# Two merge units moved forward in the list of stage 1 of a hybrid decoder block

## The chip, the core and the metric

The kernel runs on one core of one Trainium2 chip. The metric is the device time of one execution in microseconds (us). Times of single instructions are in us or ns, counted from the start of the profiled span.

## What is computed

A decoder block works on x of 1024 tokens by 1024 channels in float32. Cut to the parts that matter here:

```python
h = rmsnorm(x, norm_mix_g)
q, kv, nsa_g, u, merge_g = split(h @ w_in)         # 512, 768, 24, 512, 2048 columns
y_a = nsa(q, rope(q), compress(k_c), compress(v_c), k_s, v_s, k_w, v_w, gates) @ w_attn_branch
y_ssm = gelu(s5(u, ...))                           # 32 groups, state 64, a scan over the tokens
y_b = (y_ssm @ w_ssm_val) * sigmoid(y_ssm @ w_ssm_gate)
g_a, g_b = split(merge_g)
x = x + (sigmoid(g_a) * y_a + sigmoid(g_b) * y_b) @ w_out
x = x + square(relu(rmsnorm(x) @ w_up)) @ w_down
return rmsnorm(x, norm_final_g)
```

The merge gates `merge_g` are a product of the normed input with 2048 columns of `w_in`. They depend on nothing else and are not read before the two branches are joined.

## The kernel before

The kernel has three stages. Nearly every large product is made of three matmuls (high by high, low by high, high by low halves of float32 operands), so each weight is first cast to its high half on ACT (L111) and its low half is found by a subtraction (L112), on POOL for most weights.

**Stage 1** norms the input, transposes it into eight tiles hT, makes the u projections and then works through a list of units, the string DENSE (L50, `dense`, L618 to L638):
- `s`: one of eight batches of four state-space groups (`s5_prep`, `s5_main`). Tables and weights are made on VectorE, with sines on ACT, four transposes (pw, L513), small products (L520, L541, L542, L557 to L560), a scan on VectorE, and GELU on VectorE (L570 to L574). The batch is given to the scheduler with a priority 1200 instructions ahead (HP).
- `k`: one projection for the compressed keys or values (`kv_unit`).
- `c`: one compression MLP (`compress`), with a priority 600 ahead (HC).
- `a`, `b`: the query projection and the key, value and gate projection of one of the two key heads (`qkv_half`): eight blocks of 24 matmuls into tile ps_a, each block evacuated on ACT, rotated on POOL (L384 to L387), transposed (L402, L432) and split on ACT and VectorE (L410, L411, L429, L434, L435).
- `m`: one merge unit (`merge_steps`, L139 to L157): one weight of 128 by 1024, two halves of 24 matmuls of 512 columns each (L150, tile ps_m), a tanh on ACT (L156, tile mst) and a store to mg_d (L157). It needs nothing of VectorE.

The list gives the order in which instructions are handed to a scheduler. It keeps a time model of the engines and lets each engine take, of the instructions that are ready, the one of the best priority; priorities follow the order of the list, save for the units that stand ahead. What results is a fixed order for every engine and for SP's DMA queue. Sixteen merge units exist in all. N1 = 5 of them stand in DENSE; the first three (ND) use the three banks of the pool dps, the others the single bank of mps. Ten more (NM) are fillers of stage 2, handed out two matmuls at a time between attention products, the first 48 matmuls (PRE) ahead of it; the last one opens stage 3. Weights come through two raw slots (NR) and four weight slots.

**Stage 2** is the attention of 16 pairs of key head and block. Its first loads (L672 qT, L681 kT, L683 vt) wait for SBUF that stage 1 has given up. **Stage 3** joins the branches and runs the MLP, with a hand-written order.

Of the kernel before, what the change touches and what calls it, by code (L numbers as in the profile page):

```python
# [46 lines left out]
ATQ, MGQ, DB, MI, PW = 1, 1, 1, 0, 6  # L47
DP1, SP1, XP1, NKQ, NVV, NQT, QL = 3, 2, 2, 2, 2, 3, 1
ND3, E4, S4B, AHEAD = 5, 5, 2, 5
DENSE = 'ssksmkcssscsabasbmmmm'  # L50
N1 = DENSE.count("m")
MORDER = [f for i in range(8) for f in (i, 8 + i)]
EPS = 1e-6
# [12 lines left out]
def hybrid_block(ctx: ExitStack, tc: tile.TileContext, a: dict, out: bass.AP, dbg=None):  # L66
# [108 lines left out]
    with ExitStack() as st1:  # L175
# [446 lines left out]
        def dense(x):  # L622
            i = count[x] = count.get(x, -1) + 1
            if x == "s":
                with tc.high_priority(offset=HP) if HP else ExitStack():
                    s5_main(i, s5_prep(i))
            elif x == "k":
                kv_unit(i)
            elif x == "c":
                with tc.high_priority(offset=HC) if HC else ExitStack():  # L630
                    compress(i)
            elif x == "m":
                merge_unit(MORDER[i], dps if i < ND else None)
            else:
                qkv_half(i, "ab".index(x))

        for x in DENSE:
            dense(x)  # L638
# [869 lines left out]
```

## Time and profile before

| what | value |
|---|---|
| median of 3 runs | 1561.51 us (1561.37 to 1562.64) |
| the profiled execution | 1559.56 us, span 1557.5 us |
| TensorE (PE) busy | 1513.8 us, 97% |
| VectorE (DVE) busy | 1053.8 us, 68% |
| ACT, POOL busy | 747.7 us, 446.4 us |

Busy time of PE is the union of its matmuls, whose ends are modelled. PEld is the weight load, which overlaps PE. In a timeline each row is start, length, engine, line, operation, output and inputs, shapes and count; a bracket names the idle time just before it and the instruction that ended it. In a table by stretch each row is the stretch, its length, then busy time and count of each engine, the granted TensorE clock, the busy share of the DMA engines and GB/s.

### The profile page before, as it was taken

Reading aid. Unit: us, or ns where it says so; the run is one execution under the profiler, and the core shown is the slowest. Engines: PE = TensorE matmul, PEld = TensorE weight load, DVE = VectorE, ACT = ScalarE, POOL = GpSimd, SP = SyncE. Lnnn points to the kernel's source line nnn. Section 1 sums busy time; section 2 is a strip of 40 time slices with the busy share of each in tenths; the row PEclk is TensorE's granted clock in tenths of the full one; section 3 lists DMA queues with packets and bytes.
Section 4 is the critical chain, followed back from the end, with each engine's and each line's share of the span. In section 5 each row is a group of like instructions: output and inputs, shape, how many; then the busy total and the mean of one; then the engine's idle time right before and its main releaser. Section 6 shows DMA issues by size and latency. Waiting matters only on the chain. (4 is left out here: it accounts for less than half of the span.)

```text
span 1557.5 us, 22364 instructions
## 1 busy us (share of the span) xinstructions
PE 1513.8 (97%) x7938; PEld 1272.8 (82%) x7938; DVE 1053.8 (68%) x1867; ACT 747.7 (48%) x1548; POOL 446.4 (29%) x431
## 2 busy tenths in 40 slices
PE   7999999999999999999999979999999999999996
PEld 6789999888888888888888867888888778888885
DVE  7995977358987978565542568555555467757576
ACT  6343444347677766532221455555555444444452
POOL 3114535211011011000000034444444355445453
PEclk9999999999999999999999999999999999999998
DMA  6434455652123111363342214444443677533533
GB/s 234 134 95 156 142 165 183 180 159 63 59 59 115 39 54 49 135 233 108 122 159 84 82 44 172 164 149 149 149 149 122 197 272 235 174 109 109 188 109 122
DMA packets 113503, 211.07 MB, mean 136 GB/s; under 512 B 14704, under 2 KB 49520, under 8 KB 113392
## 3 DMA queue, kind: packets, MB, share of 16 engines
q1 hardware_dynamic: 104176, 192.87, 37.9%
q10 hardware_dynamic: 9216, 16.78, 3.1%
q8 instruction: 62, 1.02, 0.3%
q14 instruction: 49, 0.40, 0.1%
HBM read 139.36 MB, written 68.16 MB: 133 GB/s over the span
## 5 line engine op out<-in xcount | busy, mean ns | idle before, releaser
L1373 PE MATMUL pg<-w 128*128 128x512 f32 x1344 | 309.0, 392 | 4.3 <-DVE w L1246 3.4
L1373 PEld LDWEIGHTS pg<-w 128*128 128x128 f32 x1344 | 253.3, 189 | 59.8 <-DVE w L1246 5.3
L150 PE MATMUL ps_m<-hT,w 128*128 128x512 f32 x768 | 215.3, 400 | 0.4 <-ACT mst L156 0.3
L1244 POOL TENSOR_TENSOR w<-raw,w 128x512 fp32r<-128x512 f32 x112 | 153.3, 1372 | 161.0 <-ACT w L1243 159.8
L1243 ACT CAST w<-raw 128x512 fp32r<-128x512 f32 x112 | 69.5, 620 | 165.3 <-PE pg L1373 104.4
L150 PEld LDWEIGHTS ps_m<-hT,w 128*128 128x128 f32 x768 | 130.6, 188 | 21.5 <-ACT mst L156 0.8
L1062 PE MATMUL pa<-T,w 128*128 128x512 f32 x576 | 141.7, 395 | 1.1 <-POOL w L1079 1.1
L1079 POOL TENSOR_TENSOR w<-raw,w 128x1024 fp32r<-128x1024 f32 (+1 forms) x48 | 101.1, 2108 | 104.1 <-ACT w L1078 104.1
L1062 PEld LDWEIGHTS pa<-T,w 128*128 128x128 f32 x576 | 108.1, 188 | 26.7 <-POOL w L1079 1.6
L1246 DVE TENSOR_TENSOR w<-xy,w 128x512 fp32r<-128x512 f32 x64 | 87.2, 1371 | 47.4 <-ACT w L1245 32.1
L112 POOL TENSOR_TENSOR w<-raw,w 128x1024 fp32r<-128x1024 f32 (+1 forms) x27 | 71.1, 2636 | 162.4 <-ACT w L111 162.4
L769 ACT ACTIVATE p<-s_ps,sst 128x640 f32<-128x640 f32 (+7 forms) x128 | 90.0, 707 | 23.5 <-PE pt L804 13.4
L127 POOL TENSOR_TENSOR rstd<-ss,neghalf 128x1 f32<-128x1 f32 x16 | 8.8, 551 | 293.1 <-DVE ss L125 293.1
L1246 DVE TENSOR_TENSOR w<-z,w 128x512 fp32r<-128x512 f32 x48 | 59.6, 1243 | 43.4 <-ACT w L1245 41.5
L763 PE MATMUL s_ps<-kT,qT 128*128 128x512 f32 (+3 forms) x384 | 85.8, 337 | 0.2
L804 PE MATMUL pt<-ident,p 128*128 128x128 f32 x528 | 83.8, 275 | 2.1 <-DVE pl__5079 L708 1.0
L766 DVE CUSTOM_DVE_ANT_0 s_ps<-s_ps,cmask 128x256 f32<-128x256 f32 (+7 forms) x96 | 63.8, 676 | 19.6 <-PE s_ps L763 19.1
L119 PE MATMUL ps_a<-w,hT 128*128 128x256 f32 (+1 forms) x256 | 74.8, 292 | 0.0
L118 PE MATMUL ps_a<-w,hT 128*128 128x256 f32 (+1 forms) x256 | 74.6, 291 | 0.0
L120 PE MATMUL ps_a<-w,hT 128*128 128x256 f32 (+1 forms) x256 | 74.0, 289 | 0.0
L763 PEld LDWEIGHTS s_ps<-kT,qT 128*128 128x128 f32 x384 | 63.7, 189 | 11.5 <-ACT p L769 1.3
L804 PEld LDWEIGHTS pt<-ident,p 128*128 128x128 f32 x528 | 62.4, 140 | 12.4 <-PE s_ps L763 1.3
(1432 smaller groups left out, 3497.5 us busy)
## 6 DMA issues: line engine op xcount, KB each, us to landing
raw<-act_d SPq DMA_DIRECT2D x56, 512.0 KB
raw<-w_up SPq DMA_DIRECT2D x32, 512.0 KB
act_d<-ts SPq DMA_DIRECT2D x16, 1024.0 KB
raw<-w_mg SPq DMA_DIRECT2D x16, 512.0 KB
mg_d<-mst SPq DMA_DIRECT2D x32, 256.0 KB
act_d<-e SPq DMA_DIRECT2D x16, 512.0 KB
xy<-w_down ACTq DMA_DIRECT2D x32, 256.0 KB
z<-w_down ACTq DMA_DIRECT2D x32, 256.0 KB
```

The costliest lines, as they stand in the source:

```text
L118: T.matmul(ps, lhsT=wh, rhs=xh, start=first and i == 0, stop=False)
L119: T.matmul(ps, lhsT=wl, rhs=xh, start=False, stop=False)
L120: T.matmul(ps, lhsT=wh, rhs=xl, start=False, stop=last and i == n - 1)
L150: m = T.matmul(ps, lhsT=w[:, e, ks], rhs=hT[k][:, r, hs], start=k == 0 and i == 0, stop=k == KD - 1 and i == 2)
L763: T.matmul(s_ps[:, o:o + hi - lo], lhsT=qT[:, 2 + hp * 2 + j, :], rhs=kT[g, br, hf][:, e, lo - hf * 512:hi - hf * 512], start=e == 0, stop ...
L769: A.activation(pp[j][:, 0:w], row, AF.Exp, scale=-1.0, bias=st[:, 0, j:j + 1], accum_out=st[:, 2, j:j + 1])
L804: T.transpose(pt[:, i, j, :], c[hp, br][j][:, (i0 + i) * P:(i0 + i + 1) * P], ident)
L1062: T.matmul(ps, lhsT=w[:, e, ks], rhs=x[:, k], start=first and k + i == 0, stop=k == 3 and i == 2, skip_group_check=not first)
L1079: G.tensor_tensor(w[:, 1, i * n:i * n + n], x, f32(w[:, 0, i * n:i * n + n]), op=ALU.subtract)
L1244: G.tensor_tensor(w[:, 0, 1], raw, f32(w[:, 0, 0]), op=ALU.subtract)
L1246: V.tensor_tensor(w[:, 1, 1], t, f32(w[:, 1, 0]), op=ALU.subtract)
L1373: T.matmul(ps, lhsT=w[:, 0, e, bs], rhs=w[:, 1, r], start=first and q + i == 0, stop=q == 15 and i == 2, skip_group_check=not first)
```

## The change

Two of the four letters m at the end of DENSE move forward: one to the place after the fourth s, one to the place after the sixth s. The number of letters m stays 5, and their numbering, their banks and everything else in the kernel stay as they are.

```diff
@@ -47,7 +47,7 @@
 ATQ, MGQ, DB, MI, PW = 1, 1, 1, 0, 6
 DP1, SP1, XP1, NKQ, NVV, NQT, QL = 3, 2, 2, 2, 2, 3, 1
 ND3, E4, S4B, AHEAD = 5, 5, 2, 5
-DENSE = 'ssksmkcssscsabasbmmmm'
+DENSE = 'ssksmkcsmssmcsabasbmm'
 N1 = DENSE.count("m")
 MORDER = [f for i in range(8) for f in (i, 8 + i)]
 EPS = 1e-6
```

## Rows read from the trace of the kernel before

**Rows 1.** The page: busy time of TensorE, and its granted clock in 40 slices

```profile
PE 1513.8 (97%) x7938; PEld 1272.8 (82%) x7938; DVE 1053.8 (68%) x1867; ACT 747.7 (48%) x1548; POOL 446.4 (29%) x431
...
PEclk9999999999999999999999999999999999999998
```

**Rows 2.** Table by stretch: stretch, length, busy by engine, clock, DMA share, GB/s

```profile
113.70:155.00 41.30, 41.30 (x350) 40.41 (x348) 22.93 (x46) 18.01 (x45) 16.52 (x33) 1.00 0.49 149
155.00:223.00 68.00, 64.68 (x536) 62.59 (x536) 63.42 (x119) 30.40 (x87) 33.84 (x65) 1.00 0.53 157
223.00:265.00 42.00, 42.00 (x355) 41.34 (x355) 28.84 (x68) 20.38 (x62) 17.50 (x45) 1.00 0.53 164
265.00:301.00 36.00, 36.00 (x195) 30.28 (x194) 14.24 (x22) 9.92 (x20) 13.67 (x19) 1.00 0.59 170
301.00:337.00 36.00, 35.62 (x182) 29.65 (x181) 14.59 (x63) 16.21 (x50) 6.46 (x6) 1.00 0.67 201
```

**Rows 3.** Timeline of TensorE: its waits after 113 us, to 340 us

```profile
192.35 0.44 PE L432 MATMUL pk<-ident,k 128*128 128x128 f32 x2 [1.26 <-DVE k L429]
...
197.01 0.66 PE L513 MATMUL pw<-ident,wq 128*128 128x128 f32 x4 [1.96 <-DVE x L546]
...
336.38 0.73 PE L150 MATMUL ps_m<-hT,w 128*128 128x512 f32 x2 [0.34 <-ACT mst L156]
```

**Rows 4.** Timeline of VectorE: long instructions, and one of ordinary length

```profile
99.86 2.52 DVE L509 TENSOR_TENSOR wq<-wq,wq 128x512 f32<-128x512 f32 x1
...
117.84 2.44 DVE L474 TENSOR_TENSOR ang<-th,cidx 128x512 f32<-128x512 f32 x1
...
184.99 0.28 DVE L429 COPY k<-k 128x256 f32<-128x256 f32 x1
...
189.74 2.56 DVE L429 COPY k<-k 128x256 f32<-128x256 f32 x1
...
193.15 3.00 DVE L574 SCALAR_TENSOR_TENSOR gz<-gz,gy 128x512 f32<-128x512 f32 x1
```

**Rows 5.** Timeline of POOL: the subtractions for weights, 99 to 196 us

```profile
99.32 2.50 POOL L112 TENSOR_TENSOR w<-raw,w 128x1072 fp32r<-128x1072 f32 x1 [14.57 <-ACT w L111]
...
115.57 4.15 POOL L112 TENSOR_TENSOR w<-raw,w 128x1072 fp32r<-128x1072 f32 x1 [8.98 <-ACT w L111]
...
151.44 2.37 POOL L112 TENSOR_TENSOR w<-raw,w 128x1024 fp32r<-128x1024 f32 x1 [1.59 <-ACT w L111]
...
154.37 2.39 POOL L112 TENSOR_TENSOR w<-raw,w 128x1024 fp32r<-128x1024 f32 x1
...
189.23 2.92 POOL L112 TENSOR_TENSOR w<-raw,w 128x1072 fp32r<-128x1072 f32 x1
...
192.58 3.03 POOL L112 TENSOR_TENSOR w<-raw,w 128x1072 fp32r<-128x1072 f32 x1
```

**Rows 6.** Timeline of TensorE: first projection, first merge of the tail, first attention

```profile
113.72 0.28 PE L118 MATMUL ps_a<-w,hT 128*128 128x256 f32 x1
...
265.24 0.40 PE L150 MATMUL ps_m<-hT,w 128*128 128x512 f32 x1
...
301.36 0.61 PE L724 MATMUL pc_ps<-kvc,qT 128*128 128x128 f32 x4
...
308.84 5.74 PE L150 MATMUL ps_m<-hT,w 128*128 128x512 f32 x24
```

**Rows 7.** Timeline of ACT: the cast of the second query weight

```profile
80.59 1.05 ACT L111 CAST w<-raw 128x1024 fp32r<-128x1024 f32 x1 [1.58 <-PE ps_k L120]
```

**Rows 8.** Timeline of SP's queue: stage 1's last stores, stage 2's first load

```profile
277.88 8.09 SPq L157 DMA_DIRECT2D mg_d<-mst  x2
...
289.88 2.46 SPq L566 DMA_DIRECT2D y_d<-gz  x4
...
294.17 0.32 SPq L672 DMA_DIRECT2D qT<-q_d  x1
```

**Rows 9.** Table by stretch, the merge matmuls (L150) alone: PE, PEld busy

```profile
265.00:301.00 36.00, 28.91 (x119) 22.15 (x120) 1.00 0.59 170
301.00:337.00 36.00, 29.86 (x125) 22.55 (x123) 1.00 0.67 201
```

## The prediction

> **What bounds the kernel now.** I began with the busy shares and the slices of the page [rows 1]. TensorE is busy for 1513.8 of 1557.5 us and the granted clock is nine tenths of full speed (2.4 GHz) or more in 39 of the 40 slices, so the span holds 1557.5 - 1513.8 = 43.7 us in which TensorE does nothing. The change moves TensorE's work and takes none away. It can gain only idle time, and only idle time that the moved units can fill.
>
> Next comes the table by stretch for the end of the first stage [rows 2], to see which idle time that is. From 113.7 to 155 us TensorE is full and VectorE is busy 22.93 of 41.30 us. From 155 to 223 us VectorE is the tight engine, 63.42 of 68.00 us, and TensorE idles 68.00 - 64.68 = 3.32 us. From 223 to 301 us TensorE is full again, although VectorE has only 14.24 us of work in the last 36 us. From 301 to 337 us it idles 0.38 us. So in the whole reach of the change TensorE idles 3.7 us. The rest of the 43.7 us lies at the launch, at the hand-over to the MLP and at the tail, which the order of stage 1 does not touch.
>
> Then the TensorE timeline says where the 3.3 us are: two waits, 1.26 us before the key transposes and 1.96 us before a state-space transpose, both released by VectorE [rows 3], 3.22 us together. VectorE's timeline shows why it was late: a key copy that takes 0.28 us at 184.99 takes 2.56 us at 189.74, and a GELU product takes 3.00 us at 193.15 [rows 4]. Both stretched instructions lie against a POOL subtraction for the low halves of the next weights (189.23 and 192.58 us, 2.92 and 3.03 us long) [rows 5]. The trace has that pattern before as well: 2.52 us at 99.86 and 2.44 us at 117.84 on VectorE [rows 4], beside POOL's subtractions at 99.32 and 115.57 [rows 5], and there TensorE did not wait.
>
> That is a lock in the rows: a VectorE instruction of 0.28 us ends when POOL's ends. The Trainium skill, page "SBUF — State Buffer", section "Who interferes with whom", states it as an exclusive lock of a port pair that VectorE and GpSimd share, held for a whole instruction; the trace agrees (2.56 against 0.28 us).
>
> **The change, part by part.** Two letters m leave the end of DENSE; one goes after the fourth s, the other after the sixth. The number of m stays 5, so N1, MORDER and the banks chosen by ND are untouched: the moved units are the second and third, which use the three dps banks before and after. No instruction is added or removed: the same 96 matmuls, 2 weight loads and casts, 2 POOL subtractions, 4 tanh, 4 stores.
>
> *TensorE.* A half unit of 24 matmuls takes 5.74 us [rows 6]; four of them are 22.5 us with a little overlap. The s groups carry a priority 1200 ahead and the compressions one 600 ahead, so both still go before the moved units; what the units overtake is the dense work behind them, the four query and key projections a, b, a, b. Now these begin at 113.72 us, right after the second k, and the first unit of the tail starts at 265.24 [rows 6]. After the change the two units run from about 113.7 us, and the projections start and end some 22 us later. TensorE was full from 113.7 to 155 us and stays so: cost 0, gain 0.
>
> *Weights, ACT.* The weights come through four slots and are cast as slots come free, in the order of DENSE: two for k, one for the first m, two for a. The last of these five stands at 80.59 us, 33 us ahead of the projection that begins at 113.72 [rows 6, 7]. In the new order the two moved units take the places of the two query weights, so they too are ready well before 113.7 us. Their cover is those 33 us; nothing is charged. The query weights take the next two places, at about 98 and 115 us, and are wanted at about 140 us.
>
> *Stage 2's start.* The attention's first loads leave at 294.17 us, after the last state-space group's stores at 289.88 [rows 8]; the first attention matmul follows at 301.36 [rows 6]. If the s chain ends where it does now, what TensorE sees from 296 us on is the same: of the 36 us from 265 to 301, 119 merge matmuls take 119 x 5.74 / 24 = 28.5 us and the last s work 7.5 us [rows 6, 9], so the last projection ends at about 265 + 22.5 + 7.5 = 295 us, and after it come two units of the tail and the first filler unit, which stand at that time now, too. The second group's keys come late but the first blocks, all of the first group, don't read them. The one bank of mps serves four halves in a row in both orders. Cost 0.
>
> *VectorE and POOL.* Here is the term that decides. The POOL subtractions follow the release of weight slots, and these move with the projections. Before, the query weights of the second pass were subtracted at 151.44 and 154.37 us [rows 5], where VectorE was little used, and the key weights at 189 and 193 us, in the full stretch. With the projections 22 us later the first pair falls at about 175 to 180 us and the second at about 212 to 216 us: both inside the stretch in which VectorE is 93% busy [rows 2]. The pair of the first key weights leaves the full stretch before 120 us for the light one, but it cost TensorE nothing. So the 3.22 us that I know should come back at the second pair, and the first pair is new. Its price is bounded by the pairs of the trace: 0 (the pair at 99 and 116 us, where TensorE's fill asked nothing of VectorE) and 3.22 us (the pair at 189 and 193 us, where the fill was a key projection). The new pair lies at the change from a query to a key projection, nearer to the second; as only its last part is key work I take the half, 1.6 us. An end below 0 has no reason.
>
> *SP's queue.* The four stores of the moved units now stand in SP's queue ahead of the compression's loads, the Toeplitz windows and the query stores. A store waits for its tanh and holds what is behind it: now the worst is 8.09 us for two at 277.88 [rows 8]. In the new place the bounds are 0 and 8.09 us, on the state-space chain and not on TensorE; TensorE has the whole of the projections as cover, so I take 0 here and keep the rest for a rival.
>
> Sum against the profiled execution's 1559.56 us (span 1557.5 and 2.06 around it): -3.22 + 3.22 + 1.6 = +1.6, or 1561.2. The median of the runs shown is 1561.51, 1.95 above that execution, so the same sum gives **1563.1, say 1563.0 us**. A measurement of this kernel tells about 0.2%, 3.1 us, from no change: this counts as the same.
>
> **Rivals.** *The waits go (faster).* The units bring 22.5 us of TensorE work that needs nothing of VectorE. If the scheduler spreads them through the stretch from 155 to 223 us instead of spending them before it, both waits fill up, and the 0.34 us at 336.38 [rows 3] may go too: 3.22 + 0.38 = 3.6 us, 1561.51 - 3.6 = 1557.9. For it: the merges lie now where VectorE is 40% busy [rows 2]. Against it: by their priority the units are spent by 150 us. The Trainium skill, page "Perfetto Trace Analysis", section "Identifying the Most-Contended Engine", recommends interleaving regimes with different bounds, and by that rule this rival would be the outcome; the trace agrees only so far as there are 3.3 us to win. Chance 0.25.
>
> *The chain ends late and the attention starts without cover (slower).* One mechanism: the s chain is what the first attention loads wait for [rows 8]. If held stores or POOL's locks delay it by x us, the attention starts x later while TensorE goes on with the tail. In the 36 us after 301 us the tail gives 125 matmuls, 29.86 us of busy time [rows 9], and covers the attention's slow rise, which otherwise offers TensorE some 6 us of work. Each us of x takes one from that cover. It decides from a delay of about 3 us, where the halves in mps also begin to follow each other with no other work between them (0.34 us was seen for one [rows 3]). For x I take the store's 8.09 us [rows 8] as the upper end: with no slack at all 1561.5 + 8 = 1569.5, with half of it made up 1565.5. For it: the last two s groups now share VectorE with the key projection, which before was over at 265 us. Against it: from 265 to 301 us VectorE has room, 14.24 of 36 us. Chance 0.30.
>
> *The order does not change.* The scheduler takes what is ready, so the units might sit at the end as before: 1561.5. The early casts speak against it; 0.05, within the same.
>
> **How the numbers follow.** Likeliest, with the rearranged waits of about the same size: 0.40, own range 1560 to 1565, 1563.0 at its middle; with the unchanged order 0.45 for within 0.2%. Faster by over 0.2% 0.25, slower by over 0.2% 0.30. The range runs from 1557.0 (all 3.6 us, and a little in the attention) to 1570.0 (a full 8 us of lost cover).
>
> **What would show it.** In the changed profile: L150 matmuls at about 113 to 150 us; the query projection's start near 140 us; POOL's subtractions inside VectorE's full stretch, with VectorE instructions stretched to some 2.5 us beside them and TensorE waits of 1 to 2 us released by VectorE; the first attention matmul still near 301 us. The forecast is wrong if TensorE has no wait over 1 us between 113 and 300 us, or if the first attention matmul comes after 305 us and TensorE idles more than 3 us before 345 us.

## The result, and the profile after

The change takes 1573.2 us (median of 4 runs, 1570.65 to 1574.74) against 1562.08 us for the kernel before on the same chip: ratio 1.0068, 95% interval 1.0055 to 1.0081, so slower by 8.6 to 12.6 us. The forecast was 1563.0 us in a range that ended at 1570. The profiled execution took 1570.65 us with a span of 1568.7, 11.2 us over the span of before. In what follows a ratio is turned into microseconds by 1561.5.

The first two fences are a line of the page and the table by stretch of the changed kernel (stretch, length, then busy time and instructions of PE, PEld, DVE, ACT and POOL, granted clock, DMA share, GB/s), against [rows 1, 2]:

```profile
PE 1518.9 (97%) x7938; PEld 1276.0 (81%) x7938; DVE 1056.2 (67%) x1867; ACT 748.4 (48%) x1548; POOL 443.6 (28%) x431
```

```profile
113.70:155.00 41.30, 41.30 (x264) 37.15 (x262) 18.23 (x28) 10.85 (x19) 11.23 (x11) 1.00 0.49 148
155.00:223.00 68.00, 64.54 (x516) 61.56 (x515) 61.04 (x120) 31.79 (x91) 26.68 (x64) 0.97 0.46 132
223.00:265.00 42.00, 42.00 (x361) 41.20 (x360) 25.39 (x53) 19.36 (x50) 17.48 (x37) 1.00 0.51 154
265.00:301.00 36.00, 33.15 (x262) 32.27 (x261) 25.56 (x51) 13.52 (x47) 14.63 (x36) 0.95 0.46 147
301.00:337.00 36.00, 33.03 (x158) 26.63 (x158) 9.26 (x30) 12.87 (x33) 14.41 (x19) 1.00 0.78 246
```

Three things differ. TensorE's idle time from 155 to 223 us is what it was, 3.46 us for 3.32. From 265 to 337 us it is 2.85 + 2.97 = 5.82 us where it was 0.38. And in two of these stretches the granted clock is below 1.00, where before all five had 1.00. VectorE's column points to the reason: from 113.7 to 155 us its work fell from 22.93 to 18.23 us, from 265 to 301 us it rose from 14.24 to 25.56 us. The units that ask nothing of VectorE were spent where VectorE had room, and the projections, which do ask something of it, moved to where TensorE must wait for it.

TensorE's timeline names the waits (start, duration, instruction; in brackets the idle time ahead of it and what ended it), against [rows 3, 6]:

```profile
113.88 1.98 PE L150 MATMUL ps_m<-hT,w 128*128 128x512 f32 x8
...
181.25 0.49 PE L558 MATMUL py<-cGsG,vv 128*128 128x128 f32 x2 [0.93 <-DVE cGsG L553]
...
184.02 0.70 PE L560 MATMUL py<-cGsG,vw 128*128 128x128 f32 x2 [1.90 <-DVE cGsG L554]
...
271.88 0.66 PE L513 MATMUL pw<-ident,wq 128*128 128x128 f32 x4 [2.83 <-DVE wq L509]
...
309.56 0.41 PE L432 MATMUL pk<-ident,k 128*128 128x128 f32 x2 [1.42 <-DVE k L429]
...
316.98 0.68 PE L724 MATMUL pc_ps<-kvc,qT 128*128 128x128 f32 x4 [1.44 <-issue]
```

The first attention matmul comes at 316.98 instead of 301.36 us. The first two waits and the 2.83 us stand beside stretched VectorE instructions, and those beside POOL's subtractions for low halves. Here are VectorE's rows and then POOL's, to hold against [rows 4, 5]:

```profile
178.86 2.34 DVE L553 TENSOR_TENSOR cGsG<-gg,sinTcosT 128x512 f32<-128x512 f32 x1
181.12 2.84 DVE L554 TENSOR_TENSOR cGsG<-gg,sinTcosT 128x512 f32<-128x512 f32 x1
...
264.83 2.76 DVE L508 TENSOR_TENSOR wq<-B,pi 128x512 f32<-128x512 f32 x1
267.51 3.72 DVE L551 TENSOR_TENSOR_SCAN gg<-rr,x 128x128 f32<-128x128 f32 x4
...
272.31 0.69 DVE L553 TENSOR_TENSOR cGsG<-gg,sinTcosT 128x512 f32<-128x512 f32 x1
272.92 0.68 DVE L554 TENSOR_TENSOR cGsG<-gg,sinTcosT 128x512 f32<-128x512 f32 x1
```

```profile
177.92 5.49 POOL L112 TENSOR_TENSOR w<-raw,w 128x1024 fp32r<-128x1024 f32 x2 [0.41 <-ACT w L111]
224.49 3.42 POOL L112 TENSOR_TENSOR w<-raw,w 128x1072 fp32r<-128x1072 f32 x1 [1.73 <-ACT w L111]
228.28 2.48 POOL L112 TENSOR_TENSOR w<-raw,w 128x1072 fp32r<-128x1072 f32 x1
263.34 6.50 POOL L112 TENSOR_TENSOR w<-raw,w 128x1024 fp32r<-128x1024 f32 x2 [2.16 <-ACT w L111]
301.79 2.40 POOL L112 TENSOR_TENSOR w<-raw,w 128x1024 fp32r<-128x1024 f32 x1 [1.25 <-ACT w L111]
304.91 2.40 POOL L112 TENSOR_TENSOR w<-raw,w 128x1024 fp32r<-128x1024 f32 x1
```

The products of L553 and L554 take 0.69 and 0.68 us at 272 us, 2.34 and 2.84 beside the pair of the second query weights. The pair at 263.34 us is for the two merge units that are left in the tail (the units m behind the projections). The kernel before did the same two subtractions at the same time, and beside one of them a key copy took 2.44 us. Rows of the kernel before, of POOL, VectorE and TensorE:

```profile
264.20 2.40 POOL L112 TENSOR_TENSOR w<-raw,w 128x1024 fp32r<-128x1024 f32 x1 [0.47 <-ACT w L111]
267.73 2.37 POOL L112 TENSOR_TENSOR w<-raw,w 128x1024 fp32r<-128x1024 f32 x1
...
267.81 2.44 DVE L429 COPY k<-k 128x256 f32<-128x256 f32 x1 [1.21 <-POOL k L387]
...
269.22 3.02 PE L150 MATMUL ps_m<-hT,w 128*128 128x512 f32 x12
```

TensorE had no wait there: up to 269 us it had the end of the last projection and products of the state-space groups whose inputs were ready, and then twelve matmuls of the tail's merges, until the copy was done.

The two falls of the clock come with the waits of 1.90 and 2.83 us (the same table of the changed kernel in slices of 2 us; the granted clock is the third number from the right):

```profile
182.00:184.00 2.00, 0.12 (x1) 0.00 (x0) 2.00 (x2) 0.00 (x0) 1.49 (x3) 1.00 0.00 0
184.00:186.00 2.00, 1.98 (x9) 1.99 (x10) 1.87 (x5) 0.00 (x0) 0.00 (x0) 0.54 0.06 23
186.00:188.00 2.00, 2.00 (x12) 1.95 (x11) 1.93 (x3) 0.00 (x0) 0.00 (x0) 0.61 0.97 291
...
270.00:272.00 2.00, 0.12 (x1) 0.12 (x2) 1.97 (x6) 0.00 (x0) 1.28 (x6) 1.00 0.42 141
272.00:274.00 2.00, 1.98 (x13) 1.76 (x13) 1.94 (x4) 1.67 (x5) 0.00 (x0) 0.72 0.32 129
274.00:276.00 2.00, 2.00 (x11) 2.00 (x10) 1.16 (x4) 1.25 (x6) 0.86 (x4) 0.50 0.63 208
276.00:278.00 2.00, 2.00 (x17) 1.82 (x17) 0.32 (x2) 0.31 (x1) 0.00 (x0) 0.92 0.90 309
```

TensorE was busy 0.12 of 2 us, and then ran at the lower of its two levels, 1.2 GHz, for 2 x (0.46 + 0.39) = 1.7 us and 2 x (0.28 + 0.50 + 0.08) = 1.7 us worth of lost time. The waits of 1.42 and 1.44 us had no fall behind them.

SP's queue shows what the attention now stands behind (issue time, duration), against [rows 8]:

```profile
296.94 2.45 SPq L566 DMA_DIRECT2D y_d<-gz  x4
...
310.91 0.32 SPq L436 DMA_DIRECT2D k_d<-kTs  x1
313.14 0.31 SPq L672 DMA_DIRECT2D qT<-q_d  x1
```

Before, the state-space chain's stores, with one merge store behind them, were the last ahead of the attention's first load. Now the last is a key store, 14 us behind that chain's.

**The sum of the two profiled executions.** From 113.7 us to the first matmul of the MLP TensorE idles 13.0 us, before 6.6: +6.4, of which 2.83 + 1.42 + 1.44 = 5.7 between 265 us and the first attention matmul and 0.7 in the 43 us behind it. The clock's falls add 3.4. That makes 9.8 of the 11.4 us by which the MLP starts later; the other 1.6 us is matmul time spread over many groups, which these rows don't place.

### The profile page after: what moved, and what is told of

It is laid out like the page before. It is cut to its first block, busy times and chain, and to the rows that moved or that the text cites. A ratio compares the mean times of both kernels' runs of the same rounds, so it can differ in the third digit from the quotient of the medians.

```text
span 1568.7 us, 22371 instructions
## 1 busy us (share of the span) xinstructions
PE 1518.9 (97%) x7938; PEld 1276.0 (81%) x7938; DVE 1056.2 (67%) x1867; ACT 748.4 (48%) x1548; POOL 443.6 (28%) x431
## 5 line engine op out<-in xcount | busy, mean ns | idle before, releaser
L150 PE MATMUL ps_m<-hT,w 128*128 128x512 f32 x768 | 216.1, 400 | 0.1
L150 PEld LDWEIGHTS ps_m<-hT,w 128*128 128x128 f32 x768 | 130.3, 189 | 20.6 <-ACT mst L156 0.6
```

Source lines behind the costliest of these rows:

```text
L150: m = T.matmul(ps, lhsT=w[:, e, ks], rhs=hT[k][:, r, hs], start=k == 0 and i == 0, stop=k == KD - 1 and i == 2)
```

## The experiments

Two theories: **locks** (POOL's subtractions hold VectorE, TensorE waits for it and the clock falls behind the wait) and **hand-over** (projections end next to the attention's start, whose loads stand behind the last key store). Cover is TensorE's work that is ready to run while VectorE or a load is late. In the diffs DENSE is the order string, and `lo=None` puts the subtraction on VectorE.

**Two units directly ahead of the last key projection.** Nothing is done early, so the locks of the full stretch stay where they were.

```
-DENSE = 'ssksmkcssscsabasbmmmm'
+DENSE = 'ssksmkcssscsabasmmbmm'
```

> The two units stand just ahead of the last key projection, so that everything up to about 240 us is ordered nearly as before and only the end of the stage is as in the changed kernel (two units behind the last projection). Theory A, the hand-over: the last key projection now ends at about 302 us, the attention's first loads wait for its last store, and TensorE has too little left to do; it costs the 4.5 us of extra TensorE waits that the changed kernel's trace has from 301 to 350 us. It expects 1562 + 4 to 5 = 1566 to 1567 us and the first attention matmul after 312 us. Theory B, the locks: the loss lies in POOL's weight subtractions that fall into VectorE's full stretch, with TensorE waits and a fall of its clock behind them; nothing of that is moved here before 240 us, so 1561 to 1563 us.

Measured: 1567.26 us, ratio 1.0044 (1.0031 to 1.0057), 6.9 us slower. TensorE's timeline of this run:

```profile
193.35 0.44 PE L432 MATMUL pk<-ident,k 128*128 128x128 f32 x2 [1.21 <-DVE k L429]
...
197.88 0.75 PE L513 MATMUL pw<-ident,wq 128*128 128x128 f32 x4 [1.84 <-DVE x L546]
...
304.76 0.41 PE L432 MATMUL pk<-ident,k 128*128 128x128 f32 x2 [1.62 <-DVE k L429]
...
312.45 0.68 PE L724 MATMUL pc_ps<-kvc,qT 128*128 128x128 f32 x4 [1.70 <-issue]
```

The first two are the waits of before [rows 3]; the last two are new, and are those of the change at 309.56 and 316.98 us. So this order costs without any unit being early. The 6.9 us are not the hand-over alone: a later run with the late subtractions on VectorE puts that at 2.5 us. The profiled execution, 1570.92 us, also has the granted clock fall behind the wait of 1.84 us and again at 345 us.

**Only the first of the two units early.**

```
-DENSE = 'ssksmkcssscsabasbmmmm'
+DENSE = 'ssksmkcsmsscsabasbmmm'
```

> Only one unit moves; the projections shift by 11 us and three units stay at the end. Theory A expects a third unit of cover to hide most of the hand-over: 1562 to 1564 us, the first attention matmul at about 306 us. Theory B expects other meetings of POOL and VectorE than in either kernel, anywhere from 0 to 6 us: 1562 to 1568 us, with each TensorE wait over 0.8 us beside a VectorE instruction stretched by a subtraction. If both were simply proportional to the units moved, 1567.5 us.

Measured: 1569.54 us, 1.0051 (1.0039 to 1.0063). One unit costs three quarters of what two cost. From 155 to 223 us TensorE idles 5.05 us, more than in either kernel, and the first attention matmul comes at 306.18 us with a wait of 2.27 us behind it.

**The two units behind the seventh s**, right ahead of the first query projection.

```
-DENSE = 'ssksmkcsmssmcsabasbmm'
+DENSE = 'ssksmkcssscsmmabasbmm'
```

> The two units stand behind the seventh s, right ahead of the first query projection, and not among the s groups. If what matters is that the units overtake the projections, and the priority of the s groups makes their place among these meaningless, the time is that of the changed kernel: 1571 to 1575 us, with the units again at 114 to 148 us. If their place among the s groups matters, it is nearer to the kernel before: below 1567 us.

Measured: 1571.99 us, 1.0071 (1.0059 to 1.0083): the change again, with its waits (0.93, 1.90 and 2.41 us). By the priority of the s groups only what stands ahead of the projections counts, not the place among the letters s.

**The first two filler units' subtractions on VectorE** (those at 301.79 and 304.91 us), in the changed kernel.

```
-        w = weights(wpool, a["w_mg"][f], S, lo=G.tensor_tensor)
+        w = weights(wpool, a["w_mg"][f], S, lo=None if f in MORDER[5:7] else G.tensor_tensor)
```

> The changed kernel with the low halves of the first two filler weights subtracted on VectorE and not on POOL; TensorE's and ACT's orders stay the same, row by row. In the changed kernel those two subtractions (2.40 us each, at 301.8 and 304.9 us) stand in POOL's queue ahead of the last block's rotation. Theory A expects the last key copy some 4 us sooner, the wait of 1.42 us at 309.6 gone, the first attention matmul at about 313 us, and 1.5 to 3 us gained: 1570 to 1572 us against 1573.2. Theory B, which puts the loss at 180 and 270 us, expects no change: 1573 us. In both the waits at 181 to 184 us and at 272 us stay, each with its fall of the clock.

Measured: 1572.2 us, 1.0072 (1.006 to 1.0084), no different from the change. The key wait of 1.42 us is gone, one of 0.47 us for ACT stands there, and the attention still starts at 316.4 us. The time alone doesn't clear these two subtractions: a wait of 1.19 us for a load at 236.92 us is new in this run, and the state-space transpose behind the tail's pair runs at 273.02 us, 1.1 us later than in the change. From there to the first attention matmul the run is 1.7 us shorter. So these subtractions have a part in the hand-over, and a wait of 1.05 us ahead of the first attention matmul is left without them.

**The tail units' subtractions on VectorE** (the pair at 263.34 us): the line above with `MORDER[3:5]`.

> The changed kernel with one edit: the two subtractions for the two merge units left in the tail run on VectorE and no longer on POOL (6.50 us for the two at 263.34 us). Lock theory: the VectorE instructions of 2.76 and 3.72 us at 264.83 and 267.51 us shrink, TensorE's wait of 2.83 us before a state-space transpose goes, and the fall of the granted clock at 272 to 278 us with it (1.7 us): 4.5 us less than the change, 1568.7 us. Rival, the wait is the state-space chain's own (it would be late there with or without the lock): the wait stays at over 2 us and the time within 1.5 us of the change.

Measured: 1568.24 us, 1.0039 (1.0024 to 1.0055), so 0.0029 or 4.5 us less than the change (1.4 to 7.7 by the two intervals). VectorE's rows and the table by stretch of this run:

```profile
265.23 1.20 DVE L112 TENSOR_TENSOR w<-raw,w 128x1024 fp32r<-128x1024 f32 x1
...
266.92 1.13 DVE L508 TENSOR_TENSOR wq<-B,pi 128x512 f32<-128x512 f32 x1
267.96 1.61 DVE L551 TENSOR_TENSOR_SCAN gg<-rr,x 128x128 f32<-128x128 f32 x4
269.50 1.20 DVE L112 TENSOR_TENSOR w<-raw,w 128x1024 fp32r<-128x1024 f32 x1
```

```profile
265.00:301.00 36.00, 36.00 (x290) 35.04 (x289) 25.22 (x57) 16.61 (x53) 12.70 (x39) 1.00 0.53 163
301.00:337.00 36.00, 33.24 (x157) 26.86 (x156) 10.37 (x33) 11.61 (x29) 11.33 (x16) 1.00 0.84 256
```

L508 takes 1.13 us instead of 2.76, the scan 1.61 instead of 3.72, the wait of 2.83 us is gone and the clock stays at 1.00: 2.83 + 1.7 = 4.5 us, as expected. The first attention matmul comes 4.0 us earlier, at 312.99 us. The idle time from 301 to 337 us stays (2.76 us). Two costs, then, and the lock is one of them.

**The second query weights' subtractions on VectorE** (the pair at 177.92 us).

```
-            ws = [weights(wpool, a["w_q" if c == 0 else "w_kv"][g, j], 4 * n, lo=G.tensor_tensor if QG else None) for j in range(2)]
+            ws = [weights(wpool, a["w_q" if c == 0 else "w_kv"][g, j], 4 * n, lo=None if (g, c) in ((1, 0),) else G.tensor_tensor) for j in range(2)]
```

> The changed kernel with one edit: the two subtractions that make the low halves of the second pass's query weights run on VectorE (1.22 us each by the fill weights of an earlier run) and no longer on POOL (5.49 us for the two at 177.92 us). Lock theory: the two VectorE products of 2.34 and 2.84 us at 178.86 and 181.12 us shrink to some 0.6 us, TensorE's waits of 0.93 and 1.90 us go, and with them the fall of the granted clock at 184 to 188 us (1.7 us): 4.5 us less than the change, 1568.7 us. Rival, VectorE is simply full: from 181.2 to 203.9 us it is busy 22.17 of 22.70 us, so 2.44 us more work on it make TensorE wait as long as the lock did; then the time is within 1.5 us of the change, 1572 to 1574.

Measured: 1572.21 us, 1.0067 (1.005 to 1.0084): the time is the rival's, the cause only in part. The waits of 0.93 and 1.90 us go, and others come, 1.81 us for VectorE at 200.31 us, where no subtraction runs on POOL, and 2.24 us at 229.47 us. The latter is another lock: the key weights' subtractions moved from 224 to 221 us, and beside them VectorE's instructions take 2.58 and 3.68 us. Taking away one lock here moved the wait.

**Query, tail and filler weights together.** Both lines above, with `MORDER[3:7]`.

> The changed kernel with the subtractions of the second pass's query weights, of the two tail units and of the first two filler units on VectorE. Lock theory with the hand-over beside it: both waits and both clock falls go (9.0 us) and 0.6 us of the last key wait: 1573.2 - 9.6 = 1563.6 us; the first attention matmul stays some 14 us behind the last key projection, with 2 to 3 us of idle TensorE ahead of it. If the hand-over cost nothing by itself, the time would be that of the kernel before less its own two waits, about 1558. If the locks cost nothing, 1572.

Measured: 1569.52 us, 1.0041 (1.0028 to 1.0054), between the values that the theories gave. The tail's wait is gone; from 223 to 265 us TensorE idles 5.14 us, 1.16 and 2.33 us of it beside the key weights' subtractions that this run leaves on POOL. It doesn't separate lock and hand-over.

**The kernel before with the second key weights' subtractions on VectorE**: the second line above, with `((1, 1),)`.

> The kernel before with one edit: the subtractions of the second pass's key weights (2.92 and 3.03 us on POOL at 189.23 and 192.58 us) run on VectorE. Lock theory: the copy of 2.56 us and the product of 3.00 us shrink, TensorE's waits of 1.26 and 1.96 us go: 3.2 us less than the kernel before, 1558. Rival, VectorE is full there (63.42 of 68.00 us): 2.4 us more work on it and the waits stay, within 1 us of the kernel before.

Measured: 1559.51 us, 0.9987 (0.9978 to 0.9996), 2.0 us faster. That lies between the two values. The waits of 1.26 and 1.96 us are gone, but 0.46 us for VectorE at 221 us and 1.25 us at 269 us come in their place: about half of the lock's price is given back. The wait at 269 us follows the tail's pair of subtractions (here at 262.80 us, with VectorE instructions of 2.84 and 2.47 us beside it), so in the old order too that pair costs nothing only as the instructions happen to fall.

**Two units fewer behind the projections, none early**, as filler in the attention instead.

```
-SB, CB, OB, NM, LA, PB = 2, 2, 1, 10, 2, 4
+SB, CB, OB, NM, LA, PB = 2, 2, 1, 12, 2, 4
-DENSE = 'ssksmkcssscsabasbmmmm'
+DENSE = 'ssksmkcssscsabasbmm'
```

> The kernel before with two merge units fewer behind the projections and none early (DENSE ends in two m and N1 is 3; NM goes from 10 to 12, so that the two units are done as filler inside the attention). Locks, state-space chain and projections stay as they were. Cover theory: what the change costs at the hand-over (6 us, as the run with the units ahead of the last projection alone measured) is the missing merge work between the last projection and the attention; then TensorE idles 3 us or more between 284 and 345 us and the time is 4 to 6 us over the kernel before, 1565.5 to 1568. Late-key theory: what costs is that the last key projection and its store stand directly ahead of the attention's first loads; they do not here, so the time is within 1.5 us of the kernel before, 1560.5 to 1563.5.

Measured: 1567.65 us, 1.0041 (1.0028 to 1.0053), 6.4 us slower with locks, chain and projections in their old places. The idle time is 2.51 us from 301 to 337 us (before 0.38), among it 1.24 and 0.73 us behind the first attention matmul at 303.76 us, and 3.3 us from 347 to 585 us (before 2.2); the profiled execution, 1570.93 us, also has two falls of the clock, at 198 and at 314 us. The time is what the cover theory gave, so the units behind the projections were worth something where they stood. How much of the 6.4 us that is, this run doesn't show: it changes the filler inside the attention too.

**The change with two more units in the tail**, and with the tail's subtractions on VectorE besides.

```
-SB, CB, OB, NM, LA, PB = 2, 2, 1, 10, 2, 4
+SB, CB, OB, NM, LA, PB = 2, 2, 1, 8, 2, 4
-DENSE = 'ssksmkcsmssmcsabasbmm'
+DENSE = 'ssksmkcsmssmcsabasbmmmm'
```

> The changed kernel with two more merge units at the end of the tail (N1 is 7, NM is 8): the two early units stay where the change puts them, and four units again stand behind the projections. Cover theory: the idle time of the hand-over goes (1.42, 1.44 and 0.71 us and the small gaps, 3.6 us in all, and what follows): 4 to 6 us less than the change, 1567 to 1569. Late-key theory: the first attention matmul still comes some 14 us behind the last key projection, but TensorE is fed meanwhile, so 3 us of gain at most, 1570 to 1572. If the locks alone made the loss, 1572 to 1574. The filler may run out some 10 us before the attention ends; if that costs, it shows as idle time near 660 us.

> The same, with the subtractions of the first two tail units on VectorE as well. If lock and hand-over are separate costs they add: 1573.2 - 5.0 (measured for the subtractions alone) - 4 to 6 = 1562 to 1564, as good as the kernel before. If both cure the same wait, no better than the better one of the two, 1567 to 1568.

Measured: 1584.77 us, 1.0142 (1.0126 to 1.0158), and 1580.33 us, 1.0114 (1.0101 to 1.0128). All theories missed by over 10 us. The first of the two runs, TensorE's timeline:

```profile
309.36 0.41 PE L432 MATMUL pk<-ident,k 128*128 128x128 f32 x2 [1.42 <-DVE k L429]
...
316.84 0.68 PE L724 MATMUL pc_ps<-kvc,qT 128*128 128x128 f32 x4 [1.49 <-issue]
```

The filler runs out and TensorE idles 7.1 us from 585 to 720 us (busy 127.91 of 135.00), around the end of the attention, where the change idles 0.5 us. That drowns the time of both runs, but the hand-over can still be read in the trace: the waits of 1.42 and 1.49 us stand as they stood, although two more units were waiting to be done. The key transpose and the first attention matmul stand ahead of the next half unit in TensorE's order, and in the timeline that half begins only behind them. Only what follows gained, 0.45 us idle in the 43 us behind the first attention matmul for 1.30 in the change. So a cover theory that counts units is wrong for the 2.9 us ahead of the attention, and right for the 0.8 us behind it. The subtractions on VectorE are worth 0.0028 here, 0.0029 in the run without the two units.

**The late subtractions off POOL, in three orders.** The kernel before, the change, and the order with the units ahead of the last key projection, all three with the second query and key weights' and six merge units' subtractions on VectorE: `((1, 0), (1, 1))` and `MORDER[1:7]` in the lines above. From 155 to 301 us POOL then has no subtraction for a weight; the rotations stay on it.

> The kernel before with the subtractions of the second pass's query and key weights and of all merge units from the second to the seventh on VectorE. Lock theory: besides what the key weights alone gave (1559.5 against 1562.4 us) the POOL subtractions at 232, 264 and 268 us go, beside which VectorE instructions were stretched without TensorE waiting: 1558 to 1560. Rival, VectorE is full from 155 to 223 us and each microsecond of work moved onto it comes back as a TensorE wait: 1561 to 1563.

> The changed order, with all the subtractions on VectorE that the last run of the kernel before had there (second query and key weights, merge units two to seven): against that run (1557.6 us) only the order of DENSE differs, and against the change (1573.2 us) only the engine of the subtractions. If the whole loss of the change is locks, it comes out level with that run: 1557 to 1559.5. If the hand-over costs by itself (the last key projection's store ahead of the attention's loads, TensorE's queue standing at the first attention matmul), that is left: idle time of 1.5 to 3 us ahead of a first attention matmul after 312 us, 0.7 us behind it, and a fall of the granted clock or none: 3 to 6 us more than that run, 1560.5 to 1563.5. If moving the subtractions only shifts the locks and fills VectorE, as with the query weights alone, 1568 to 1572.

> The same split of the subtractions, with the two units directly ahead of the last key projection instead (the order that cost 6 us with the locks in place). Here locks, early place and full stretch are out of it, and the hand-over alone is left: by the hand-over theory 3 to 6 us over the kernel before with the same split (1557.6 us), 1560.5 to 1563.5, with the first attention matmul some 14 us behind the last key projection and TensorE idle 1.5 us or more before it. If the locks made the loss, 1557 to 1559.5.

Measured: the order of before 1557.62 us, 0.9972 (0.9961 to 0.9984), the fastest kernel of this study; the changed order 1562.27 us, 1.0008 (0.9999 to 1.0017); the units ahead of the last key projection 1560.69 us, 0.9988 (0.9979 to 0.9997). The table by stretch for the old order, for the changed one, and the last two stretches for the units ahead of the last key projection, each cut at its first attention matmul (304.24, 308.32 and 307.51 us):

```profile
155.00:223.00 68.00, 67.81 (x568) 65.96 (x567) 63.26 (x126) 32.17 (x92) 26.73 (x62) 1.00 0.55 157
223.00:265.00 42.00, 41.86 (x334) 40.33 (x334) 29.46 (x67) 19.66 (x60) 14.91 (x44) 1.00 0.53 161
265.00:304.24 39.24, 38.50 (x206) 32.12 (x205) 14.89 (x27) 9.44 (x17) 3.74 (x10) 1.00 0.56 167
304.24:347.24 43.00, 42.68 (x229) 35.44 (x228) 22.33 (x99) 24.59 (x83) 9.69 (x9) 1.00 0.61 186
```

```profile
155.00:223.00 68.00, 65.64 (x542) 63.14 (x541) 61.36 (x124) 34.97 (x97) 25.17 (x64) 1.00 0.50 141
223.00:265.00 42.00, 40.60 (x345) 39.53 (x344) 26.67 (x54) 18.08 (x47) 11.89 (x36) 1.00 0.49 148
265.00:308.32 43.32, 41.47 (x300) 38.26 (x298) 24.90 (x55) 16.66 (x52) 11.86 (x42) 1.00 0.59 186
308.32:351.32 43.00, 41.81 (x225) 34.91 (x226) 21.83 (x97) 22.45 (x81) 9.66 (x9) 1.00 0.66 196
```

```profile
265.00:307.51 42.51, 40.29 (x289) 37.06 (x288) 23.91 (x52) 13.95 (x42) 12.76 (x41) 1.00 0.48 148
307.51:350.51 43.00, 41.87 (x208) 35.16 (x209) 19.60 (x90) 19.82 (x69) 8.72 (x7) 0.92 0.61 185
```

With these locks away the new order still costs 1.0008 / 0.9972 = 1.0036, 5.6 us; with them it cost 1.0068, 10.6 us. So the locks make 5.0 us of the loss, and the tail's pair alone made 4.5. By the intervals each of these differences is known to 2 or 3 us. The order makes the rest, and the rows show where: 2.36 us idle for 0.19 from 155 to 223 us (1.80 of it one wait for VectorE at 198.02 us), 1.40 for 0.14 to 265 us (for the loads of a compression's weights), 1.85 for 0.74 up to the first attention matmul and 1.19 for 0.32 in the 43 us behind it, 5.4 us more in all. The units ahead of the last projection alone cost 0.9988 / 0.9972, 2.5 us: the hand-over by itself. Its rows agree, 2.22 us idle for 0.74 and 1.13 for 0.32, 2.3 us more, with the first attention matmul 14.1 us behind the last projection and a wait of 1.75 us ahead of it. So of the order's 5.6 us less than half lies at the hand-over; the rest lies ahead of 265 us.

## Why the prediction was wrong

Two steps of the sum failed. *VectorE and POOL*, priced at 1.6 us, stopped one pair of subtractions short: the tail's pair, not in the sum, gave 4.5 us when it was taken off POOL alone. *Stage 2's start*, priced at 0, cost 2.5 us by itself. The two falls of the clock, 3.4 us that the sum did not have, came behind the waits of the first step. Some 3 us more of what the order costs without the locks lie ahead of 265 us, and their cause stays open.

**TensorE, 113 to 155 us:** right. The units run from 113.88 us and TensorE stays full.

**Weights:** right for the moved units, which were never waited for. But the step followed the slots only to the projections. The next pair in the same row of slots, for the tail, is the one that costs most.

**VectorE and POOL:** the mechanism was right, two of the three places wrong. "The 3.22 us that I know should come back at the second pair": that pair fell at 224 and 228 us, behind the full stretch, and cost nothing. The new pair, taken at half of 3.22, cost 0.93 + 1.90 = 2.83 us, near its upper bound. And the tail's pair, which the text did not price, cost 2.83 us of wait. By the traces it was the cover that went: when those subtractions ran before, TensorE had ready work and then merges, and the change put the second key projection and a state-space transpose there. No run moved that cover alone. The waits between 113.7 and 301 us came to 6.3 us where 4.8 were forecast.

**The clock** was not in the sum. With 3.4 us in the profiled execution it weighs as much as the 3.0 us that the change added to TensorE's idle time up to 301 us (6.3 for 3.3).

**Stage 2's start, "cost 0":** this step failed too. It argued that the first attention blocks don't read the second group's keys. They don't, but their first load leaves 2.2 us behind the issue of the last key store (313.14 and 310.91 us). In the ten traces with an "issue" wait ahead of the first attention matmul that load leaves 2.1 to 3.3 us behind the last key store, and the matmul comes 3.4 to 3.8 us behind the load. That the load waits for the store is inferred from this and not shown alone; with the query, tail and filler weights together on VectorE it left 5.7 us behind, so something else held it there. The projections ended at 302 us, not 295, in part by the locks: without the tail's they ended at 298.4 us. The change paid 1.42 + 1.44 us ahead of the first attention matmul and 0.7 us behind it.

**The rivals.** "The chain ends late and the attention starts without cover" had the place right and the cause wrong: it was not the s chain but the last key projection behind it, and two more units behind the projections did not cure it. Its price, 4 to 8 us, is near the 5.6 us that the order cost without the locks, but by luck: only 2.5 us of these lie at the hand-over. No case held hand-over and locks together. "The waits go" fell, because the units were spent by 147 us and none was left for the full stretch. The Trainium skill, page "Perfetto Trace Analysis", section "Optimization Strategy" (the prediction names the section ahead of it), says that interleaving regimes with different most-contended engines may improve performance. The traces don't speak against that; the prediction took the change for such an interleaving, and it took one away: [rows 2] had the projections, which need VectorE, in the stretch where VectorE was busy 22.93 of 41.30 us, and the merges, which don't, beside the state-space chain's end.

**The mark set beforehand** for a wrong forecast was met: a first attention matmul after 305 us, at 316.98, and more than 3 us of idle time before 345 us. Two slips in the working changed nothing: the middle of 1560 to 1565 is 1562.5, and the attention from 337 to 585 us held 2.3 us of idle time that the text gave to other places.

**What stays open:** the 1.6 us of matmul time in the sum, and the share of chance in the clock's falls. The run with the units ahead of the last projection had the old waits of 1.21 and 1.84 us and a clock of 0.58 and 0.57 behind them from 198 to 202 us; in the profiled execution of before no fall followed its 1.26 and 1.96 us. What decides whether a fall follows a wait is not shown. For the new order's waits ahead of 265 us without the locks the rows name VectorE and a load, but no run took either away.

## What to carry to other kernels

Work that asks nothing of the second busiest engine is cover, and cover has a place: before it is moved, look up which stretched instruction, late chain or hand-over stands beside it in the trace, even where that costs nothing now. Follow a moved block's successors through every resource that it shares, buffer slots included, until they are back in their old times. Where VectorE is full, removing one lock can hand its wait on to the next place, as two runs here did in part; taking the ten late subtractions off POOL together made the kernel before 0.28% faster (0.9972).

## What the runs showed of the hardware that was not expected

A wait of 2 to 3 us can cost TensorE more than its length: in the change the granted clock fell to the lower level behind 1.90 and 2.83 us, and each fall took 1.7 us more. With the 2.83 us wait gone the clock held 1.00 in the same stretch; the 4.5 us that the run gained fit wait and fall together, but the times by themselves don't tell 4.5 from 2.8. The length of one wait doesn't settle it: no fall followed 2.27 us (first of the two units alone, 309.13 us) or 2.33 us (query, tail and filler weights together, 230.24 us), and one followed a wait of 0.71 us (units ahead of the last key projection, 343.06 us).

The same two subtractions on VectorE take 1.20 us each where POOL's row shows 6.50 us for the pair; although VectorE does 2.4 us more work, the two instructions that had stood beside the pair lost 1.6 and 2.1 us of their length.
